# Ten of twelve heads' q, k, v by seven products of halves, turned back on TensorE

## The chip, the cores and the metric

One core of a Trainium2 chip runs one launch of the kernel. The metric is the device time of that launch in microseconds, the median of three runs. TensorE is called PE below, VectorE DVE, ScalarE ACT, GpSimd POOL and SyncE SP.

## What is computed

One decoder layer over 2048 tokens of width 1024, in fp32. The parts that the change touches, cut from the reference:

```python
h = (rms_norm(x, norm_w) * (1.0 + scale[:, None]) + shift[:, None]).astype(dt)
z = h @ w_in                      # 1024 x 10240
a, b, g_conv, q, k, v, g_attn, m_conv, m_attn = jnp.split(z, SPLIT_POINTS, axis=-1)
u = depthwise_causal_conv(a * jax.nn.sigmoid(b), conv_w, conv_b)      # 31 taps
...
q = rope(rms_norm(q, q_norm_w).astype(dt), positions)      # 12 heads of 128
k = rope(rms_norm(k, k_norm_w).astype(dt), positions)
for g, (window, dilation) in enumerate(((128, 1), (512, 4), (2048, 16))):
    sl = slice(g * HEADS_PER_GROUP, (g + 1) * HEADS_PER_GROUP)        # four heads
    o_g, l_g = dilated_window_attention(q[:, :, sl], k[:, :, sl], v[:, :, sl], window, dilation)
...                               # the groups merged by softmax of l_g, then gates and projections
```

## The kernel before

**The input h.** The rows of x are normalised, transposed on PE and kept in SBUF as "quarters": 4 blocks of 128 channels by 512 tokens, each as a high part and a low part (`hT_hi`, `hT_lo`). A product of two fp32 matrices is three matmuls: high by high, high by low, low by high. h is also written to memory (`h_d`).

**Stage one: units.** A unit `u` is one head. `GROUPS = (1, 2, 0)`: units 0 to 3 have dilation 4, units 4 to 7 dilation 16, units 8 to 11 dilation 1. For each unit and each block `j` of 128 tokens, `project_step` issues 24 matmuls of 128 x 384 (eight channel blocks by three terms, line 371) into one PSUM bank `pz`, which holds q, k and v of the block with tokens on partitions. Then ACT squares q and k for the norm (L388), POOL takes the inverse root (L114, L115), DVE scales (L402) and turns by the angles (L409 to L412). Units 0 to 7 write the block to memory (`qkv_d`) and their attention reads it back with a stride (`lqk`, `lv`); units 8 to 11 use it from SBUF.

Two places as they stand, the terms of a block's 24 matmuls and the seven products of a quad:

```python
        terms = [(k, a, w[k]) for k in range(KC) for a, w in ((hi, wh), (hi, wl), (lo, wh))]
...
            nc.tensor.matmul(pz[:, :width], part(a, k, P * j, P), w[:, :width], start=(m == 0), stop=(m == 23))
...
    PRODUCTS = (("A11", "B11"), ("A12", "B21"), ("S2", "T2"), ("S1", "T1"), ("S3", "T3"), ("S4", "B22"), ("A22", "T4"))
...
            terms = [t for k in range(4) for t in ((wh[:, k], ah[:, k]), (wh[:, k], al[:, k]), (wl[:, k], ah[:, k]))]
```

**Attention.** A block of attention has four steps, five in group 0: transposing q and k (`ptq`, L436), scores (`ps`, L451) with the softmax on DVE and ACT (L461, L463), transposing the weights (`ptp`, L468), times v (`po`, L500), and, where u is 8 or more, the merging of the three groups (`weigh`, L476 to L484) and the turn of the result (`pta`, L491). One step per projection step, inserted between its matmuls, is what `Flow` deals out. The tags z, s, o and t of the PSUM pool have two banks each; all eight are used.

**Stage two: quads.** The rest of `w_in` is computed with channels on partitions, for pairs of 128-column blocks, in two halves of 1024 tokens. One pair and one half is a job, or quad: seven products of quarters instead of eight (`PRODUCTS`), 12 matmuls of 128 x 512 each (L897), with ACT copying partial results out of PSUM (L903) and DVE and POOL adding. One product of one job is called a slot. 22 jobs per half: 12 gates, 2 of the attention gate, 8 of the convolution's input (`ab`); 44 jobs, 308 slots. `column_steps` loads the four weight blocks, forms the differences and splits them into high and low (L860 on ACT, L861 on DVE or POOL), seven slots ahead. In the first half the differences are stored (`t_d`), in the second read again. The sums of quarters of h come from `s_d`; between the halves, two jobs at a time are run alternately while the quarters of the second half land and are split (L725, L726). The 31-tap convolution runs on DVE beside the quads: `run_conv` emits 2.9 of its 800 small steps per slot in the first half, 3.1 in the second.

**Stage three.** The output projections of attention (`ya`) and convolution (`yc`), and the last projection by seven products (`oa`, `ob`, `oc`).

PE's order is the program's own, written out by hand (`tc.manual_schedule`). On the other engines a planner orders instructions by its estimate of when they can run; each engine then works its list strictly in that order.

Of the kernel before, what the change touches and what calls it, by code (L numbers as in the profile page):

```python
# [54 lines left out]
def tile_hybrid_block(  # L55
# [19 lines left out]
    def bank(tag, name):  # L75
        return psum.tile([P, 512], F32, tag=tag, name=name)

    qkv_d = {u: dram.tile([S, 3, P], F32, name=f"qkv{u}_d") for u in range(2 * NH)}
# [10 lines left out]
    wo_d = dram.tile([7, 4, P, 512], F32, name="wo_d")  # L89
# [144 lines left out]
    def part(x, k, t0, w, nk=1):  # L234

        q = x[k // 4, t0 // 512]
        ks = k % 4 if nk == 1 else slice(k % 4, k % 4 + nk)
        return q[:, ks, t0 % 512 : t0 % 512 + w]
# [137 lines left out]
    def tokens_tiles(n):  # L376

        return wk.tile([P, 2, P], F32, tag="lqk", name=f"lqk{n}", bufs=3), wk.tile([P, P], F32, tag="lv", name=f"lv{n}", bufs=8)

    def project_step(u, j, cs, wts, hooks, hold=False):  # L380

        n = f"{u}_{j}"
        pz = bank("z", f"pz{n}")
        z_tokens(pz, 384, *wts, j, hooks, u == 0 and j == 0)
        sq = wk.tile([P, P], BF16, tag="sq", name=f"sq{n}", bufs=1)
        st = wk.tile([P, 8], F32, tag="sta", name=f"st{n}", bufs=4)
        for i in range(2):
            nc.scalar.activation(sq, pz[:, P * i : P * i + P], AF.Square, scale=1.0 / math.sqrt(P),  # L388
                                 accum_out=st[:, i : i + 1])
        if GROUPS[u // NH]:  # L390
            qkv = wk.tile([P, 3, P], F32, tag="qkv", name=f"qkv{n}")
            tq, tv = qkv[:, :2], qkv[:, 2]
        elif hold:
            held = wk.tile([P, 3, P], F32, tag="qkv", name=f"qkv{n}")
            tq, tv = qkv = held[:, :2], held[:, 2]
        else:
            tq, tv = qkv = tokens_tiles(n)
        nc.scalar.activation(tv, pz[:, 256:384], AF.Copy)
        rsqrt_cols(st[:, 2:4], st[:, 0:2], 2, st[:, 4:6])
        qk = wk.tile([P, 4, 64], F32, tag="qk", name=f"qk{n}", bufs=1)  # L400
        for i in range(2):
            nc.vector.scalar_tensor_tensor(qk[:, 2 * i : 2 * i + 2].rearrange("p a b -> p (a b)"),  # L402
                                           pz[:, P * i : P * i + P], st[:, 2 + i : 3 + i], wqk[:, i, :],
                                           op0=ALU.mult, op1=ALU.mult)
        t3 = wk.tile([P, 2, 2, 64], F32, tag="t3", name=f"t3{n}", bufs=1)
        t1 = tq.rearrange("p a (b c) -> p a b c", b=2)
        cosb = cs[:, j, 0, :][:, None, :].to_broadcast([P, 4, 64])
        sinb = cs[:, j, 1, :][:, None, :].to_broadcast([P, 4, 64])
        nc.vector.tensor_tensor(t3.rearrange("p a b c -> p (a b) c"), qk, sinb, op=ALU.mult)  # L409
        nc.vector.tensor_tensor(t1.rearrange("p a b c -> p (a b) c"), qk, cosb, op=ALU.mult)  # L410
        nc.vector.tensor_sub(t1[:, :, 0, :], t1[:, :, 0, :], t3[:, :, 1, :])
        nc.vector.tensor_add(t1[:, :, 1, :], t1[:, :, 1, :], t3[:, :, 0, :])  # L412
        return qkv

    def strided(u, j):

        src = qkv_d[u].rearrange("(n i r) a c -> r n i a c", n=4, r=4)[j // 4, j % 4] if GROUPS[u // NH] == 1 else \
            qkv_d[u].rearrange("(i r) a c -> r i a c", r=16)[j]
        qk, v = tokens_tiles(f"{u}_{j}")
# [4 lines left out]
    def attend_step(u, j, qkv, state, hold=False):  # L424
# [8 lines left out]
        def turn_qk():  # L433
            pt = bank("t", f"ptq{n}")
            for i in range(2):
                nc.tensor.transpose(pt[:, P * i : P * i + P], qk[:, i], ident)  # L436
            if g == 0 and not hold:
                fetch()
            if hold:
                qkT = wk.tile([P, 3, P], F32, tag="qkv", name=f"qkT{n}")[:, :2]  # L440
            else:
                qkT = wk.tile([P, 2, P], F32, tag="qkT", name=f"qkT{n}", bufs=3)
            nc.scalar.activation(qkT.rearrange("p a b -> p (a b)"), pt[:, :256], AF.Copy)  # L443
            box["kv"] = ([] if first or hold else [state["prev"]]) + [(qkT, v)]
# [3 lines left out]
        def scores():  # L448
            ps = bank("s", f"ps{n}")
            for i, (kt, _) in enumerate(box["kv"]):  # L450
                nc.tensor.matmul(ps[:, P * i : P * i + P], box["q"][:, 0, :], kt[:, 1, :], start=True, stop=True)  # L451
            o = box["o"] = wk.tile([P, ACC_W], F32, tag="osb", name=f"osb{n}", bufs=5)
            if g == 0:
                st = box["st"] = mp.tile([P, 5, NG], F32, tag="stm", name=f"stm{n}", bufs=4)
                if hold:
                    fetch()
# [3 lines left out]
            sm = box["sm"] = wk.tile([P, 256], F32, tag="sm", name=f"sm{n}")  # L460
# [4 lines left out]
        def turn_p():  # L465
            pt = bank("t", f"ptp{n}")
            for i in range(nk):
                nc.tensor.transpose(pt[:, P * i : P * i + P], box["sm"][:, P * i : P * i + P], ident)  # L468
            pT = box["pT"] = wk.tile([P, 256], F32, tag="pT", name=f"pT{n}")
# [16 lines left out]
        def turn_o():  # L486
            if j % 2 == 0:
                return
            pt = bank("t" if u == NG * NH - 1 and j in (13, 15, 1, 3) else "o", f"pta{n}")
            for b, o in enumerate((state["even"], box["o"])):  # L490
# [630 lines left out]
    for at in range(7):  # L1121
        prepare(at)
# [451 lines left out]
```

## Time and profile before

| | |
|---|---|
| median of three runs | 2398.8 us (2398.56 to 2399.97) |
| profiled execution | 2401.62 us, its span 2399.8 us |
| stage one, heads | about 46 to 1099 us |
| stage two, quads | 1099 to 1960 us |
| stage three | 1960 to 2400 us |
| mean granted PE clock | 0.993 |
| moved by DMA | 378.6 MB, 158 GB/s over the span |

PE's busy time is a sum of overlapping instructions, so the spacing between starts is what counts. The stage limits are read from the first and last instructions of the lines named above.

### The profile page before, as it was taken

The page shows a single profiled execution, that of the slowest core. Times are in us where ns is not written, and L with a number is a line of the kernel's source. Part 1 is how long each engine was busy: PE and PEld are TensorE (multiplying, and loading weights), DVE is VectorE, ACT ScalarE, POOL GpSimd, SP SyncE. Part 2 cuts the span into 40 slices and gives each one's busy share as a digit, 9 for nine tenths or more (in the row PEclk, how much of TensorE's full clock was granted, in tenths as well). Part 3 has the DMA queues.
Part 4 walks back from the last instruction along what each step waited for, and adds up shares of the span by engine and source line. Part 5 has one row for each costly group of instructions (what it writes and reads, how often), then busy time and mean ns, then how long its engine had stood idle before and what let it go on. Part 6 is the DMA issues. An engine that isn't in the chain of part 4 may idle for free.

```text
span 2399.8 us, 38725 instructions
## 1 busy us (share of the span) xinstructions
PE 2356.1 (98%) x12353; PEld 2089.2 (87%) x12353; DVE 1738.8 (72%) x4091; ACT 1022.4 (43%) x2850; POOL 842.7 (35%) x1003
## 2 busy tenths in 40 slices
PE   6999999999999999999999999999999999999999
PEld 2989999999999999998888888788888888878887
DVE  5865655655556777777699999979968778787544
ACT  4733433333444454456444444644444444332221
POOL 3421111111111111123667779656556730000221
PEclk8999999999999999999999999999999999999999
DMA  7633544555552222134545455745444579866552
GB/s 258 216 118 105 163 124 143 155 151 155 165 161 79 65 79 62 55 108 156 169 133 176 154 158 193 239 127 152 141 149 132 167 228 319 288 230 200 177 158 101
DMA packets 354105, 378.56 MB, mean 158 GB/s; under 512 B 29736, under 2 KB 251208, under 8 KB 353902
## 3 DMA queue, kind: packets, MB, share of 16 engines
q1 hardware_dynamic: 316414, 316.64, 42.4%
q10 hardware_dynamic: 37488, 59.46, 7.3%
q8 instruction: 98, 1.61, 0.3%
q14 instruction: 105, 0.86, 0.1%
HBM read 235.34 MB, written 140.64 MB: 157 GB/s over the span
## 4 chain that ended last, share of the span: by engine, by line
PE 87%; DVE 3%; DMA 2%; ACT 2%; issue 1%; POOL 1%; SPq 0%; ACTq 0%; DVEq 0%; POOLq 0%
PE pz L371 29%; PE paab L897 7%; PE yc L1203 6%; PE oa L1485 4%; PE ya L1203 4%; PE pcab L897 4%; PE pag_mc_d L897 4%; PE pag_g_d L897 3%; PE pag_ma_d L897 3%; PE po L500 3%; PE ps L451 3%; PE oc L1485 2%; PE pcg_g_d L897 2%; PE pcg_mc_d L897 2%; PE paag L897 2%; PE pbab L897 2%
## 5 line engine op out<-in xcount | busy, mean ns | idle before, releaser
L371 PE MATMUL pz<-wh_u,hT_lo 128*128 128x384 f32 x1536 | 536.8, 350 | 5.4 <-DVE hT_lo L290 3.6
L371 PE MATMUL pz<-wh_u,hT_hi 128*128 128x384 f32 x1536 | 518.7, 338 | 4.8 <-ACT wh_u L347 2.4
L371 PE MATMUL pz<-wl_u,hT_hi 128*128 128x384 f32 x1536 | 519.2, 338 | 0.4 <-DVE wl_u L350 0.4
L114 POOL TENSOR_SCALAR st<-st 128x2 f32<-128x2 f32 x192 | 48.6, 253 | 809.8 <-ACT sq L388 809.8
L402 DVE SCALAR_TENSOR_TENSOR qk<-pz,st,wqk 128x128 f32<-128x128 f32 x384 | 116.9, 346 | 270.7 <-POOL st L115 269.6
L371 PEld LDWEIGHTS pz<-wh_u,hT_hi 128*128 128x128 f32 x1536 | 291.0, 189 | 8.0 <-ACT wh_u L347 3.3
L371 PEld LDWEIGHTS pz<-wh_u,hT_lo 128*128 128x128 f32 x1536 | 290.0, 189 | 8.3 <-DVE hT_lo L290 4.6
L371 PEld LDWEIGHTS pz<-wl_u,hT_hi 128*128 128x128 f32 x1536 | 290.0, 189 | 1.6 <-DVE wl_u L350 1.1
L443 ACT ACTIVATE qkT<-ptq 128x256 f32<-128x256 f32 x192 | 73.5, 383 | 358.3 <-PE ptq L436 304.0
L975 DVE SCALAR_TENSOR_TENSOR ce<-us,pair_taps,ce 128x512 f32<-128x512 f32 x240 | 180.6, 753 | 6.5
L946 DVE SCALAR_TENSOR_TENSOR ce<-ut,chan,ce 128x512 f32<-128x512 f32 x240 | 178.7, 745 | 0.0
L861 POOL TENSOR_TENSOR slT<-wT,shT 128x512 fp32r<-128x512 f32 x107 | 143.7, 1344 | 81.0 <-ACT shT L860 81.0
L959 DVE SCALAR_TENSOR_TENSOR cq<-ut,chan,cq 128x512 f32<-128x512 f32 x208 | 155.2, 746 | 1.0
L860 ACT ACTIVATE shB<-wB 128x512 fp32r<-128x512 f32 x130 | 82.0, 631 | 162.7 <-PE paab L897 51.7
L115 POOL TENSOR_TENSOR st<-st,mhalf 128x2 f32<-128x2 f32 x192 | 137.3, 715 | 16.0
L388 ACT ACTIVATE sq<-pz 128x128 bf16<-128x128 f32 x384 | 105.6, 275 | 87.5 <-PE pz L371 78.5
L860 ACT ACTIVATE shT<-wT 128x512 fp32r<-128x512 f32 x110 | 69.4, 631 | 163.9 <-POOL wT L852 33.3
L861 POOL TENSOR_TENSOR slB<-wB,shB 128x512 fp32r<-128x512 f32 x85 | 111.0, 1306 | 77.9 <-ACT shB L860 77.4
L500 PE MATMUL po<-lv,pT 128*128 128x128 f32 x596 | 96.8, 274 | 0.0
L500 PEld LDWEIGHTS po<-lv,pT 128*128 128x128 f32 x596 | 90.9, 190 | 0.6 <-issue 0.5
L409 DVE TENSOR_TENSOR t<-qk,tab 128x256 f32<-128x256 f32 x192 | 82.4, 429 | 5.5
L861 POOL TENSOR_TENSOR slT<-wB,shT 128x512 fp32r<-128x512 f32 x57 | 75.1, 1322 | 27.5 <-ACT shT L860 27.4
(742 smaller groups left out, 6162.2 us busy)
## 6 DMA issues: line engine op xcount, KB each, us to landing
wB<-in_w_in_dram SPq DMA_DIRECT2D x154, 256.0 KB, 3.4
qkv_d<-qkv SPq DMA_DIRECT2D x128, 192.0 KB, 2.3
wT<-tT_d SPq DMA_DIRECT2D x88, 256.0 KB, 2.7
raw_u<-in_w_in_dram SPq DMA_DIRECT2D x93, 192.0 KB, 3.4
tT_d<-wB ACTq DMA_DIRECT2D x66, 256.0 KB, 2.3
lqk<-qkv_d SPq DMA_DIRECT2D x128, 128.0 KB, 2.2
acc_d<-osb SPq DMA_DIRECT2D x128, 65.0 KB, 2.0
part<-acc_d ACTq DMA_DIRECT2D x64, 130.0 KB, 2.2
```

Source lines behind the costliest of these rows:

```text
L115: nc.gpsimd.tensor_tensor(dst, scratch[:, :n], mhalf[:, :n], op=ALU.pow)
L371: nc.tensor.matmul(pz[:, :width], part(a, k, P * j, P), w[:, :width], start=(m == 0), stop=(m == 23))
L402: nc.vector.scalar_tensor_tensor(qk[:, 2 * i : 2 * i + 2].rearrange("p a b -> p (a b)"), pz[:, P * i : P * i + P], st[:, 2 + i : 3 + i], w ...
L500: nc.tensor.matmul(po[:, :P], box["pT"][:, P * i : P * i + P], vt, start=(i == 0), stop=(i == nk - 1))
L860: nc.scalar.activation(h, q[name], AF.Copy)
L861: eng.tensor_tensor(l, q[name], h.bitcast(F32), op=ALU.subtract)
L897: nc.tensor.matmul(ps, w, x, start=(m == 0 and ps.name not in first), stop=(m == 11 and not more), skip_group_check=True)
L946: stt(box["e"], e[:, 1 + j : 513 + j], chan[:, cb, 2 * j : 2 * j + 1], box["e"], op0=ALU.mult, op1=ALU.add)
L959: stt(box["o"], o[:, 2 + j : 514 + j], w, psum_o, op0=ALU.mult, op1=ALU.add)
L975: stt(dst, box["both"][:, 1 + j : 513 + j], pair_taps[:, cb, j : j + 1], box["e"], op0=ALU.mult, op1=ALU.subtract if j == 0 else ALU.add)
L1203: nc.tensor.matmul(pz, w, xx, start=(m == 0), stop=(m == len(terms) - 1))
L1485: nc.tensor.matmul(ps, y, w, start=(m == 0 and ps.name not in begun), stop=(m == 11 and not more), skip_group_check=True)
```

## The change

Only units 0 and 1 are still projected block by block (`DIRECT = 2`). For the other ten heads, 30 blocks of 128 columns become 15 pairs: for two heads, v with v, then q with k of each. They are run as quads, in two rounds: all 15 for tokens 1024 to 2047, then all 15 for tokens 0 to 1023. The gates and `ab` jobs follow for the first half and then the second, so there are 74 jobs and 518 slots.

- A head quad gives q, k, v with channels on partitions, so `turn_back` transposes them on PE in pairs of token blocks (four 128 x 128 transposes into one bank), and `finish_qk` does norm and angles for two blocks at once. Results of all heads go to memory, and all attention is read from memory.
- In the first round the split weights (high and low) are written to memory, 512 KB for each product; in the second round they are read back and not split again. That is 7 x 15 pieces.
- Attention steps and turns are dealt out by `hook`, called twice in each slot, ahead of the sixth and of the last of its 12 matmuls. A block's steps are two hooks apart (`GAP = 2`). Blocks start at 0.25 per hook in the first round, none from slot 91 to 118, then at most one per hook as the heads become ready. All of it must be done by slot 237 (`TAIL`), after which the convolution begins at 3.1 steps per slot, 3.3 in the second half.
- Landing of the other half's quarters now happens twice: at slot 91 and at slot 350. The first uses three landing buffers.
- Until `TAIL`, `pb` and `pc` of a quad share one PSUM bank of tag s, the turns have the other, and the banks of tags o and t serve all attention steps of one hook together.
- The gate row (`gate_*`) and the sums of quarters for the first half move into these slots; those for the second half (`early_sums`) are formed during unit 1. Look-ahead of the weights is six slots instead of seven.

```diff
-            for p in range(NB):
-                j = (p + 3) % NB if last_unit else p
+    DIRECT = 2
+    for u in range(DIRECT):
+        for p in range(NB):
+            j = (p + 12) % NB if u else p
...
+            project_step(u, j, cur, extra)
...
+    def turn_back(pair):
+
+        pz = bank("s", f"zt{pair[0][1]}{pair[0][2][0]}_{pair[0][3]}", 1) if lone() else bank("o", f"zt{pair[0][1]}{pair[0][2][0]}_{pair[0][3]}")
+        for a, e in enumerate(pair):
+            for i, z in enumerate(e[4:6]):
+                nc.tensor.transpose(pz[:, 256 * a + P * i : 256 * a + P * i + P], z, ident)
...
+    def finish_qk(n, j, nb, pz, to):
...
+        if nb == 2:
+            src = qk.rearrange("p a b -> p (a b)")
+            nc.scalar.activation(src, pz, AF.Copy)
+            pz = src
+        for i in range(nq):
+            nc.scalar.activation(sq, pz[:, P * i : P * i + P], AF.Square, scale=1.0 / math.sqrt(P),
+                                 accum_out=st[:, i : i + 1])
+        rsqrt_cols(st[:, 4 : 4 + nq], st[:, 0:nq], nq, st[:, 8:12])
+        for i in range(nq):
+            nc.vector.scalar_tensor_tensor(qk[:, 2 * i : 2 * i + 2].rearrange("p a b -> p (a b)"),
+                                           pz[:, P * i : P * i + P], st[:, 4 + i : 5 + i], wqk[:, i % 2, :],
+                                           op0=ALU.mult, op1=ALU.mult)
...
+        nc.vector.tensor_tensor(by_block(tq), by_block(t3), cosb, op=ALU.mult)
+        nc.vector.tensor_tensor(by_block(t3), by_block(t3), sinb, op=ALU.mult)
+        nc.vector.tensor_sub(tq[:, 0::2], tq[:, 0::2], t3[:, 1::2])
+        nc.vector.tensor_add(tq[:, 1::2], tq[:, 1::2], t3[:, 0::2])
...
-        def turn_qk():
-            pt = bank("t", f"ptq{n}")
+        def turn_qk(get):
+            pt = get("t")[:, 256:]
             for i in range(2):
                 nc.tensor.transpose(pt[:, P * i : P * i + P], qk[:, i], ident)
...
+        steps = []
+        for f in (turn_qk, scores, turn_p, values) + ((turn_o,) if g == 0 else ()):
+            steps += [f, *[lambda get: None] * (GAP - 1)]
...
             for m, (w, x) in enumerate(terms):
+                if m in ((3, 7, 11) if 201 <= slot[0] < 201 else (5, 11)):
+                    hook(m > 5)
                 nc.tensor.matmul(ps, w, x, start=(m == 0 and ps.name not in first), stop=(m == 11 and not more),
...
+    heads = []
+    for u in range(DIRECT, NG * NH, 2):
+        heads += [("v", (u, u + 1)), ("q", (u,)), ("q", (u + 1,))]
+    heads.insert(-3, heads.pop(-3))
...
+    def hook(late_half):
+        at = slot[0]
+        if at >= TAIL:
+            return
...
+        ready = sum(e[0] <= at for e in turned)
+        since[0] += 1
+        if ready > 1 and since[0] >= (3 if lone() else 2):
+            since[0] = 0
+            pair = [turned.pop(0) for _ in range(2)]
+            readers.append(turn_back(pair))
...
+        readers += [f(get) for f in main.turn()]
+        for f in readers:
+            if f:
+                f()
+        credit[0] = min(credit[0] + rate(at), 1.5)
+        if order and credit[0] >= 1 and len(waiting) < 3 and is_ready(*order[0], at):
+            credit[0] -= 1
+            u, j = order.pop(0)
+            waiting.append([2, u, j, strided(u, j)])
...
+    def lone():
+        return not any(a <= slot[0] < a + 28 for a in (begin[s1 - 2], begin[s3 - 2]))
+
+    def rate(at):
+        return 0.25 if at < begin[s1 - 2] else 0.0 if at < begin[s1] + 14 else 1.0
...
-        due += 2.9 if i < half_jobs - 2 else 1.5 if i < half_jobs + 2 else 3.1
-        count = int(due)
-        due -= count
-        run_conv(count)
+        if at > TAIL:
+            due += 3.1 if i < s3 - 2 else 1.5 if i < s3 + 2 else 3.3
+            count = int(due)
+            due -= count
+            run_conv(count)
```

In the added code `s1`, `s2` and `s3` are the numbers of the first job of the second head round, of the gates of the first half and of the second half (15, 30, 52), and `begin` gives the slot at which a job starts: `begin[s1 - 2]` is 91, `begin[s1]` 105, `begin[s3 - 2]` 350.

More of the change, by code (lines that the diff above doesn't have):

```diff
@@ L726, in quarter_split @@
         i2 = eng.tensor_tensor(l, raw, h.bitcast(F32), op=ALU.subtract)
-        if half == 0 and name == "S4":
+        if name == "S4" and eng is nc.vector and cols.stop - cols.start == 512 and s4_pinned[0]:
             tc.keep_in_program_order(i1)
@@ L915, in quad @@
         yield
+        pc = bank("s" if narrow else "o", f"pc{name}", 0 if alone else None)
         product(3, pc, True)
```

525 lines of the change are left out of this document (287 added, 238 removed).

## The prediction, on record before the changed kernel ran

> **What bounds the kernel now.** I read the page first, then the engines by stretches, then the chain of waits in order of time. The page:
>
> ```profile
> span 2399.8 us, 38725 instructions
> PE 2356.1 (98%) x12353; PEld 2089.2 (87%) x12353; DVE 1738.8 (72%) x4091; ACT 1022.4 (43%) x2850; POOL 842.7 (35%) x1003
> PE 87%; DVE 3%; DMA 2%; ACT 2%; issue 1%; POOL 1%; SPq 0%; ACTq 0%; DVEq 0%; POOLq 0%
> ```
>
> PE is busy 98% and carries 87% of the chain that ended last. Busy time overlaps between instructions, so prices must come from spacings. Four stretches (length, then busy time of PE, PEld, DVE, ACT, POOL with their instructions, then granted clock, DMA share, GB/s): the attention of group 0, the convolution beside the first half of the quads, the change of halves, the start of the last stage.
>
> ```profile
> 742.00:1096.00 354.00, 352.86 (x2340) 350.33 (x2341) 264.30 (x1080) 182.15 (x735) 66.05 (x180) 1.00 0.27 76
> 1200.00:1500.00 300.00, 299.43 (x1321) 247.69 (x1320) 281.43 (x408) 126.79 (x224) 230.21 (x188) 1.00 0.50 163
> 1500.00:1545.00 45.00, 40.55 (x167) 33.01 (x166) 43.50 (x57) 29.99 (x58) 31.17 (x22) 0.92 0.83 261
> 1960.00:2050.00 90.00, 90.00 (x402) 72.94 (x401) 66.17 (x107) 34.92 (x57) 2.90 (x4) 1.00 0.97 324
> ```
>
> PE has no gap worth the name except at the change of halves. DVE is second: 75% in group 0's attention, 94% under the convolution. The chain of waits gives lengths of unbroken matmul runs (start, length):
>
> ```profile
> 572.97 4.19 PE pz L371 x24
> 1261.53 5.44 PE pag_mc_d L897 x24
> 1536.12 5.49 PE paab L897 x12
> ```
>
> The first is one block of one unit, 24 matmuls of 384 columns, 0.174 us each. The second is two slots of a quad: 12 matmuls of 512 columns take 2.72 us, 0.227 each. The third is a slot that took double; I come back to it. PE's timeline in an attention step (start, length of the merged row):
>
> ```profile
> 800.81 0.34 PE L371 MATMUL pz<-wl_u,hT_hi 128*128 128x384 f32 x1
> 800.99 0.61 PE L500 MATMUL po<-lv,pT 128*128 128x128 f32 x4
> 801.43 0.38 PE L468 MATMUL ptp<-ident,sm 128*128 128x128 f32 x2
> 801.65 0.39 PE L451 MATMUL ps<-qkT,qkT 128*128 128x128 f32 x2
> 801.87 0.39 PE L451 MATMUL ps<-qkT 128*128 128x128 f32 x2
> 802.09 0.38 PE L436 MATMUL ptq<-ident,lqk 128*128 128x128 f32 x2
> 802.23 0.42 PE L371 MATMUL pz<-wh_u,hT_lo 128*128 128x384 f32 x1
> 802.49 0.34 PE L371 MATMUL pz<-wh_u,hT_hi 128*128 128x384 f32 x1
> ```
>
> From 800.81 to 802.49 are 1.68 us: two matmuls of 0.174 and twelve small fp32 ones, 0.111 us each, transposes and products alike, with no extra price for the break.
>
> **PE's own sum.** Removed: 10 heads x 16 blocks = 160 runs of about 4.18 us, 668.8 us. Added: 15 pairs x 2 rounds x 7 products = 210 slots of 2.72 us, 571.2 us. Added: for each pair and round 8 token blocks of 2 heads' columns, 16 transposes, 480 in all, x 0.111 = 53.3 us. The attention's own PE instructions stay the same. Sum: 571.2 + 53.3 - 668.8 = **-44.3 us**. That is the ceiling of the gain, since seven eighths of the columns are left but each must be turned. Everything else is a question of what stays hidden.
>
> **Where cover gets thin.** Group prices (busy sum, mean ns; then idle before, and what ended it), DVE and then ACT, one DMA issue on ACT and POOL's split:
>
> ```profile
> L975 DVE SCALAR_TENSOR_TENSOR ce<-us,pair_taps,ce 128x512 f32<-128x512 f32 x240 | 180.6, 753 | 6.5
> L402 DVE SCALAR_TENSOR_TENSOR qk<-pz,st,wqk 128x128 f32<-128x128 f32 x384 | 116.9, 346 | 270.7 <-POOL st L115 269.6
> L409 DVE TENSOR_TENSOR t<-qk,tab 128x256 f32<-128x256 f32 x192 | 82.4, 429 | 5.5
> L461 DVE CUSTOM_DVE_ANT_0 sm<-ps,mask 128x256 f32<-128x256 f32 x108 | 44.6, 414 | 0.0
> L470 DVE COPY pT<-ptp 128x256 f32<-128x256 f32 x108 | 44.5, 413 | 0.0
> L861 DVE TENSOR_TENSOR slB<-wB,shB 128x512 fp32r<-128x512 f32 x45 | 37.3, 828 | 21.1 <-ACT shB L860 20.9
> L484 DVE SCALAR_TENSOR_TENSOR part<-part,stm 128x128 f32<-128x128 f32 x64 | 22.8, 357 | 9.5 <-ACT part L483 9.0
> L502 DVE SCALAR_TENSOR_TENSOR osb<-po,stm,part 128x128 f32<-128x128 f32 x64 | 21.9, 344 | 0.4 <-PE po L500 0.4
> L683 DVE TENSOR_TENSOR sx<-sx,sx 128x512 f32<-128x512 f32 x32 | 21.8, 683 | 0.0
> L479 DVE TENSOR_TENSOR stm<-stm 128x3 f32<-128x3 f32 x64 | 10.4, 162 | 26.6 <-ACT stm L478 23.9
> ...
> L388 ACT ACTIVATE sq<-pz 128x128 bf16<-128x128 f32 x384 | 105.6, 275 | 87.5 <-PE pz L371 78.5 <-DVE wT L852 2.1
> L860 ACT ACTIVATE shB<-wB 128x512 fp32r<-128x512 f32 x130 | 82.0, 631 | 162.7 <-PE paab L897 51.7 <-PE pag_mc_d L897 31.0 <-PE pag_g_d L897 22.6
> L443 ACT ACTIVATE qkT<-ptq 128x256 f32<-128x256 f32 x192 | 73.5, 383 | 358.3 <-PE ptq L436 304.0 <-DVE pT L470 39.8 <-DVE lqk L412 6.8
> L463 ACT ACTIVATE sm<-sm,stm 128x256 f32<-128x256 f32 x60 | 30.4, 506 | 11.5 <-DVE stm L461 11.5
> L483 ACT ACTIVATE part<-part,stm 128x128 f32<-128x128 f32 x64 | 25.5, 400 | 5.9 <-DVE stm L482 5.5 <-ACT spare_hi L1023 0.4
> ...
> 802.08 0.33 ACTq L516 DMA_DIRECT2D part<-acc_d  x1
> ...
> L861 POOL TENSOR_TENSOR slT<-wT,shT 128x512 fp32r<-128x512 f32 x107 | 143.7, 1344 | 81.0 <-ACT shT L860 81.0
> ```
>
> *The attention's tail.* Following `hook` and `is_ready` by hand through the slots: 32 blocks start before slot 70, none until 129, the other 160 in slots 129 to 231, because a head of the second round is complete only some eight slots after its quad. 53 of group 0's 64 blocks fall into the 35 slots 196 to 230, with 12 pairs of q and k to finish, two head quads and three gate quads. There:
> PE: 35 x 2.72 + 53 x 13 x 0.111 + 48 x 0.111 = 95 + 76 + 5 = 177 us.
> DVE: a block costs 0.414 (scores) + 0.413 (copy) + 5 x 0.162 (small ones) + 0.357 + 0.344 = 2.34; a pair 4 x 0.346 + 2 x 0.683 + 2 x 0.429 = 3.61 (its 512-wide multiplications priced at L683). 53 x 2.34 + 12 x 3.61 + 10 sums x 0.683 + 6 splits x 0.828 = 179 us. Between the small ones it waits for ACT's exponential, 26.6/64 = 0.42 a block, 22 us if nothing fills it.
> ACT: a block 0.383 + 0.506 + 0.400 + 2 x 0.275 + 0.33 for the issue = 2.17; a pair 0.631 + 4 x 0.275 = 1.73; 53 x 2.17 + 12 x 1.73 + 55 copies of 512 x 0.631 + 24 issues x 0.33 = 178 us.
> All three are full, where before this attention ran at 75% DVE. 94% is the highest DVE share at which the trace shows PE unhurt, and 179/0.94 = 190: **+14 us**. Ends: +2 (DVE perfectly packed, 179), +37 (waits unfilled as well, 201/0.94 = 214). I take 14 since the planner did fill 94% under the convolution.
>
> *The second landing.* At the change of halves PE waits once and then runs a slot at half speed (who waited for whom: total, times, longest):
>
> ```profile
> PE paab L897 <- ACT spare_hi L1023: 4.4, 1, 4.4
> ```
>
> 4.4, and 5.49 - 2.72 = 2.8 in the slot that took double: 7.2 us. The change has this event twice, the new one with three landing buffers. **+7 us**; 0 if the planner hides it, 20 if ACT stands behind several late landings.
>
> *The old passage from units to quads* disappears. There PE stood 2.0 us for a bank and resumed at 0.42 instead of 0.227 a matmul:
>
> ```profile
> 1104.75 0.44 PE L436 MATMUL ptq<-ident,lqk 128*128 128x128 f32 x2 [2.00 <-DVE pT L470]
> 1104.95 0.62 PE L897 MATMUL pbg_g_d<-hT_hi,first_w 128*128 128x512 f32 x1
> 1105.37 0.63 PE L897 MATMUL pbg_g_d<-hT_lo,first_w 128*128 128x512 f32 x1
> ```
>
> The attention that held the bank is gone, but first weights must still arrive at slot 0. **-3 us** (-5 to 0).
>
> *Convolution.* The same 800 steps get 280 slots instead of 295; 0.2 more per slot x 0.753 = 0.15 us on 281.43/300 x 2.72 = 2.55: 2.70 of 2.72. **+3 us** (0 to 8).
>
> *First round.* In each stretch of seven slots in which q and k are finished, DVE has 4 x 3.61 + 3 x 0.828 + 2 x 0.683 + 3.5 blocks x 1.17 (0.414, 0.413, 0.344) = 22.4 us; PE 19 + 16 x 0.111 + 3.5 x 11 x 0.111 = 25. Covered. But a 512-wide subtraction that costs 0.683 beside the units (L683; POOL at 66.05/354 in the stretch shown) costs 0.828 at L861, where POOL is at 230/300; here POOL has nine pieces of about 1.34 a job, half its time. **+2 us** (0 to 10). [...]
>
> *Step distance.* A step came once per block, over 5 us apart; now two hooks, about 3.4 us in the first round and 5.5 in the tail, with DVE bursts of 3.6 us ahead of it. `pb` must be read within one slot since `pc` takes its bank. What hides it is the planner's order. **+3 us** (0 to 15).
>
> Gate row, sums of quarters and the doubled weight traffic I cost at nothing. The first are 32 DVE operations in slots with spare DVE. In the first round a slot of about 3.6 us moves 512 KB of split weights, about 146 KB of raw ones, 150 KB of q, k, v and 130 KB for attention, some 270 GB/s; at 324 GB/s PE was busy 90.00 of 90. On SP's queue the weights are issued six slots ahead, so a store that waits for DVE delays them within that lead; without it each slot would see a landing.
>
> Sum: -44.3 + 14 + 7 - 3 + 3 + 2 + 3 = **-18.3 us**. Against the profiled execution's span of 2399.8 us (1.8 us around it, and 2.8 above the median of the runs) this is 2381.5; applied to the median 2398.8 it gives **2381 us**.
>
> **The rivals.** *Tail bound by DVE, slower:* in slots 196 to 230 its waits stay unfilled and the two banks of tags o and t make PE stand for each hook: 214 instead of 177, +37. Pauses then reach 2 us, and the rows at 1104.75 show that such a one is followed by half speed; six of them at 2 us more are +12. With the other terms (+12) the total is -44.3 + 37 + 12 + 12 = +17, 2416 us. It decides once the tail's loss exceeds 32 us. For it: three full engines; against it: 94% was carried without loss. Chance 0.24. A landing at its upper end together with the step distance gives the same sign, 2405; chance 0.06.
> *Full cover:* DVE packs the tail, the landing hides: 2354 us. Chance 0.09.
> *Clock:* group 0's hooks put 14 small fp32 instructions after six large ones, over half of PE's time. The trace granted 1.00 from 742 to 1096 with such bursts a quarter of the time. If the share counted, half speed over the tail would add 177 us at most, about 2560; chance 0.04. [...]
> *Nothing gained:* losses of 40 to 49 leave no measurable change, within 0.2% (about 4.8 us, what a measurement of this kernel can tell from none): 0.09.
>
> **How the numbers follow.** Forecast, 5 to 35 us faster: 0.48. Faster 0.48 + 0.09 = 0.57, same 0.09, slower 0.34. The range goes from full cover, 2354, into the slower cases to 2422, which leaves out the clock and the worst landings.
>
> **What would show it.** Right: 210 new slots of 2.72 us, 480 transposes at 0.111, PE gaps only at slots 91 to 112 and 196 to 231, DVE above 90% there. Wrong: a granted clock below 0.97, PE waiting for DVE in the first round, runs of 12 matmuls longer than 2.72 outside those places, or PE standing at turns for their bank.

## The result and the profile after

The changed kernel takes 2468.6 us, median of four runs (2464.97 to 2472.47), beside 2398.7 for the kernel before on the same chip (2396.47 to 2399.97). The ratio is 1.0293, 95% interval 1.0274 to 1.0311: slower by 70 us where the prediction said faster by 18, and beyond the upper end of its range, 2422.

The page of the kernel after, its span and the busy times:

```profile
span 2465.4 us, 37563 instructions
PE 2353.1 (95%) x11513; PEld 1948.4 (79%) x11513; DVE 1836.6 (74%) x3822; ACT 1167.1 (47%) x3041; POOL 1041.9 (42%) x1011
PE 65%; DVE 14%; DMA 10%; ACT 5%; issue 4%; POOL 3%; SPq 1%; POOLq 0%; DVEq 0%; ACTq 0%
```

In the chain that ended last PE fell from 87% to 65%; DVE rose from 3% to 14% and DMA from 2% to 10%: PE now stands for other engines and for transfers. The number of PE's instructions moved as the prediction had it: 12353 - 160 x 24 + 210 x 12 + 480 = 11513.

To see where PE stands we summed, stretch by stretch, the time from each of its instructions' start to the next one's, less the spacing that each has in an unbroken run (0.227, 0.174 or 0.111 us by width). We call the sum **PE's loss**; it holds standing still and half-speed matmuls (0.43 us apart after the wait at 497.11, below) alike. What is left is PE's own time: 2304.6 us before, 2261.9 after, so PE's work fell by **42.7 us**. This figure is made of instruction counts times these spacings. The loss rose from 91.8 to about 199.5 us. Together the two changes make up, to within a microsecond, the 65.6 us by which the spans of the two traces differ (2465.4 and 2399.8). By stretch:

| stretch of the kernel after | us | loss | the same places before |
|---|---|---|---|
| first two heads as units | 150 to 222 | 10.3 | 150 to 1140: 14.4 in all |
| first round, slots 0 to 90 | 222 to 586 | **55.8** | |
| landing, 91 to 117 | 586 to 684 | 18.7 | |
| second round, 118 to 195 | 684 to 1024 | 9.4 | |
| attention's tail, 196 to 230 | 1024 to 1235 | **31.8** | |
| quads beside the convolution | 1235 to 1561 | 1.4 | 0.9 |
| second landing | 1561 to 1604 | 5.4 | 7.5 |
| all the rest | | 67 | 69 |

The engines in these stretches, from the first round on (length, then busy times as in the prediction, granted clock, DMA share, GB/s):

```profile
222.00:586.00 364.00, 329.72 (x1633) 268.62 (x1634) 257.14 (x474) 186.24 (x534) 203.38 (x176) 0.96 0.82 275
586.00:684.00 98.00, 85.34 (x378) 69.40 (x377) 72.11 (x128) 54.77 (x165) 47.49 (x43) 0.92 0.77 264
684.00:1024.00 340.00, 336.72 (x2009) 292.07 (x2008) 189.57 (x689) 181.98 (x653) 51.86 (x74) 1.00 0.81 244
1024.00:1235.00 211.00, 191.12 (x1184) 162.19 (x1183) 173.85 (x682) 142.56 (x507) 81.41 (x122) 0.98 0.63 191
1235.00:1561.00 326.00, 325.25 (x1437) 268.56 (x1436) 280.99 (x429) 142.21 (x248) 244.15 (x201) 1.00 0.50 164
1561.00:1604.00 43.00, 38.10 (x169) 31.22 (x167) 42.23 (x59) 27.84 (x52) 35.35 (x25) 1.00 0.72 230
```

The first and third rows are the same sort of work, quads with q, k, v to finish. PE is busy in 329.72 of 364 us of the one and in 336.72 of 340 of the other. DVE is no fuller than 71% in either; what differs most is POOL: 203 us busy in the first, 52 in the third, where the stored weights are read again.

Groups of DVE's instructions between 225 and 580 us, after, and then the matching scaling of the kernel before in the same window:

```profile
L394 DVE SCALAR_TENSOR_TENSOR qkq<-qkq,stq,wqk 128x128 f32<-128x128 f32 x112 | 71.0, 692 | 9.0 <-POOL stq L118 8.9
L403 DVE TENSOR_TENSOR qkq<-qkq,tab 128x512 f32<-128x512 f32 x28 | 26.2, 935 | 0.6
```

```profile
L402 DVE SCALAR_TENSOR_TENSOR qk<-pz,st,wqk 128x128 f32<-128x128 f32 x134 | 40.8, 346 | 142.7 <-POOL st L115 142.7
```

The same 128x128 scaling takes 692 ns instead of 346 by the mean. The median is still 347: in slots 0 to 90, 38 of the 112 scalings take over 600 ns, up to 1452, and none of them lies between 400 and 600. So most are unhurt and a third are far longer. The scaling used to read PSUM (`pz`); now it reads ACT's copy in SBUF (`qkq`) beside `wqk` in SBUF. The timeline of the kernel after shows one pair of heads (start, length of the merged row):

```profile
490.17 1.68 POOL L832 TENSOR_TENSOR wB_make<-wB_make,wB_make 128x512 f32<-128x512 f32 x1 [0.38 <-DVE sB_make L846]
490.61 5.27 DVE L394 SCALAR_TENSOR_TENSOR qkq<-qkq,stq,wqk 128x128 f32<-128x128 f32 x4
...
491.93 1.26 POOL L832 TENSOR_TENSOR wT<-wB_make,wB_make 128x512 f32<-128x512 f32 x1
...
493.15 1.31 POOL L832 TENSOR_TENSOR wB_make<-wB_make,wB_make 128x512 f32<-128x512 f32 x1
494.43 1.30 POOL L846 TENSOR_TENSOR sB_make<-wB_make,sB_make 128x512 fp32r<-128x512 f32 x1
...
496.00 0.41 DVE L490 CUSTOM_DVE_ANT_0 sm<-turn_o_False,mask 128x256 f32<-128x256 f32 x1
...
496.45 0.51 ACT L492 ACTIVATE sm<-sm,osb 128x256 f32<-128x256 f32 x1 [4.32 <-DVE osb L490]
...
497.11 0.69 PE L497 MATMUL turn_t_False<-ident,sm 128*128 128x128 f32 x2 [5.02 <-ACT sm L492]
...
497.88 1.20 PE L891 MATMUL pav<-S_hi,sT_make 128*128 128x512 f32 x2
```

Four scalings take 5.27 us, about as long as the four POOL subtractions beside them, 5.55. The softmax's first step stands behind them in DVE's list (the last of its scores' matmuls takes 0.39 us from 488.48, the step starts at 496.00), ACT's exponential waits for it, and PE waits 5.02 us at its turn. Its next large matmuls start 0.43 us apart instead of 0.227. Where POOL pauses, the four take 1.13 us:

```profile
636.02 1.13 DVE L394 SCALAR_TENSOR_TENSOR qkq<-qkq,stq,wqk 128x128 f32<-128x128 f32 x4
```

PE's waits between 225 and 690 us carry it on (total, times, longest):

```profile
PE turn_t_False L497 <- ACT sm L492: 17.4, 10, 5.0
PE turn_o_False L531 <- DVE pT L502: 7.4, 6, 2.7
PE ztq L422 <- ACT qkq L387: 7.0, 2, 6.7
PE pcv L891 <- DVE spare_lo L904: 5.8, 2, 3.2
```

### The profile page after: what moved, and what is told of

It reads as the page before. It is cut to its first block, busy times and chain, and to the rows that moved or that the text cites. A ratio compares the mean times of both kernels' runs of the same rounds, so it can differ in the third digit from the quotient of the medians.

```text
span 2465.4 us, 37563 instructions
## 1 busy us (share of the span) xinstructions
PE 2353.1 (95%) x11513; PEld 1948.4 (79%) x11513; DVE 1836.6 (74%) x3822; ACT 1167.1 (47%) x3041; POOL 1041.9 (42%) x1011
## 3 DMA queue, kind: packets, MB, share of 16 engines
q8 instruction: 91, 1.49, 0.2%
## 4 chain that ended last, share of the span: by engine, by line
PE 65%; DVE 14%; DMA 10%; ACT 5%; issue 4%; POOL 3%; SPq 1%; POOLq 0%; DVEq 0%; ACTq 0%
PE yc L1337 7%; PE paab L891 7%; PE paq L891 4%; PE oa L1619 4%; PE pcab L891 4%; PE pag_g_d L891 4%; PE ya L1337 3%; DVE qkq L394 3%; PE pag_ma_d L891 3%; PE pcq L891 2%; PE pag_mc_d L891 2%; PE pav L891 2%; DMA part<-acc_d 2%; PE oc L1619 2%; PE pbab L891 2%
## 5 line engine op out<-in xcount | busy, mean ns | idle before, releaser
L846 POOL TENSOR_TENSOR sT_make<-wB_make,sT_make 128x512 fp32r<-128x512 f32 x108 | 148.1, 1372 | 108.3 <-ACT sT_make L845 99.6
L394 DVE SCALAR_TENSOR_TENSOR qkq<-qkq,stq,wqk 128x128 f32<-128x128 f32 x320 | 143.8, 510 | 52.4 <-POOL stq L118 51.9
L846 POOL TENSOR_TENSOR sT_again<-wT_again,sT_again 128x512 fp32r<-128x512 f32 x88 | 116.4, 1323 | 91.5 <-ACT sT_again L845 77.8
L832 POOL TENSOR_TENSOR wB_make<-wB_make,wB_make 128x512 f32<-128x512 f32 x72 | 96.5, 1341 | 58.2 <-DVE sB_make L846 53.6
L846 POOL TENSOR_TENSOR sB_again<-wB_again,sB_again 128x512 fp32r<-128x512 f32 x66 | 89.7, 1359 | 43.6 <-ACT sB_again L845 24.5
L390 ACT ACTIVATE sqq<-qkq 128x128 bf16<-128x128 f32 x320 | 98.1, 306 | 10.7 <-DVE stm L513 3.0
L374 PE MATMUL pz<-wh_u,hT_hi 128*128 128x384 f32 x256 | 90.3, 353 | 8.9 <-DVE qk L394 3.1
L374 PE MATMUL pz<-wh_u,hT_lo 128*128 128x384 f32 x256 | 89.2, 350 | 4.7 <-DVE hT_lo L293 4.6
L118 POOL TENSOR_TENSOR stq<-stq,mhalf 128x4 f32<-128x4 f32 x80 | 90.8, 1135 | 6.0
L374 PE MATMUL pz<-wl_u,hT_hi 128*128 128x384 f32 x256 | 89.5, 350 | 0.9 <-DVE wl_u L353 0.8
```

What stands on the lines that cost most here:

```text
L832: (nc.vector if first else nc.gpsimd).tensor_tensor(dst, x0, x1, op=ALU.subtract)
L846: eng.tensor_tensor(hl[:, 1], q[name], hl[:, 0].bitcast(F32), op=ALU.subtract)
```

## The experiments

**Theory A:** DVE instructions with two SBUF inputs and POOL's instructions exclude each other, whole instruction by whole instruction, and the changed scaling is newly exposed to this. **Rival B:** two hooks between the steps of attention are too few, whatever the scaling costs. The tail and the landing were tried beside them. Each ratio below is to the kernel before on the same chip in the same session.

**1. The scaling reads PSUM again (e1_psum).**

```diff
-        if nb == 2:
-            src = qk.rearrange("p a b -> p (a b)")
-            nc.scalar.activation(src, pz, AF.Copy)
-            pz = src
```

> The norm's squares and scaling of a pair read the turned q and k in PSUM, without the copy to SBUF. Theory A (exclusion: a DVE instruction with two SBUF inputs and a POOL instruction do not run side by side, so each scaling waits for a whole POOL instruction): the scaling's mean falls from 510 ns over the kernel (about 680 in the first head round) to about 350, the stretch from slot 0 to slot 91 falls from 361 us by 20 to 30, the whole kernel from 2468 to about 2435. Rival B (step distance: two hooks are too short for any burst of DVE work before them): the scaling may get shorter, but PE still stands for the softmax, slot 0 to 91 stays above 350 and the total above 2455; holding the bank longer may even add waits for the turns.

Measured: 2483.0 us (2478.0 to 2488.2), 1.0336 [1.0319, 1.0353]. DVE's group and PE's largest wait, 225 to 580 and 225 to 690 us:

```profile
L390 DVE SCALAR_TENSOR_TENSOR qkq<-ztq,stq,wqk 128x128 f32<-128x128 f32 x108 | 30.4, 344 | 28.0 <-POOL stq L118 27.8
```

```profile
PE ztq L418 <- DVE qkq L390: 43.3, 12, 6.5
```

The duration is back at 344 ns, as theory A says. But the kernel is slower, not faster: the bank with the turned q and k is now held until POOL's inverse root and DVE's scaling are done, and PE stands for it. The first round's loss is 68.2 us. ACT's copy, which exposes the scaling, is also what frees the bank; half of theory A's expectation failed. PE's waits for the exponential did fall, from 17.4 to 2.7 us, but the total is where rival B had put it, above 2455, so this run alone doesn't decide between the two.

**2. Four hooks between the first round's steps (e2_gap4).**

```diff
+        gap = 4 if slot[0] < begin[s1 - 2] else GAP
...
-            steps += [f, *[lambda get: None] * (GAP - 1)]
-        return steps[: len(steps) - GAP + 1]
+            steps += [f, *[lambda get: None] * (gap - 1)]
+        return steps[: len(steps) - gap + 1]
```

> Attention blocks that start in the first head round have their steps four hooks apart instead of two; nothing else changes. Rival B (step distance): PE's waits for the softmax (about 17 us) and for the copied weights (7) in slots 0 to 91 vanish, the stretch falls from 361 us to 330 or less, the total to about 2435. Theory A (exclusion with POOL): DVE's scaling stays at about 680 ns there, a part of the waits goes because there is time to bear them, but those for the one PSUM bank of the sums remain; the stretch falls by 10 to 20, the total to about 2450. Both expect the tail (slots 196 to 231) unchanged.

Measured: 2467.9 us, 1.0278 [1.0262, 1.0293]. PE's waits between 225 and 690 us: those for the exponential are gone, and others stand in their place:

```profile
PE pcq L892 <- DVE spare_hi L905: 9.4, 3, 5.2
PE ztq L422 <- ACT qkq L387: 8.0, 2, 7.2
PE pav L892 <- ACT spare_lo L898: 7.0, 4, 2.7
PE pcv L892 <- DVE spare_hi L905: 5.3, 1, 5.3
```

The first round still loses 52.6 us, so rival B, which had put the total at 2435, falls: a late DVE delays whatever PE needs next. Theory A's own figure for this run, 2450, was missed too.

**3. A part of POOL's work out (e3_nopool), then all of its weight work of the first round (e5_quiet).** Both replace POOL's low parts by a copy on ACT; the second also leaves out the differences of weights. The outputs of both lack these terms. The edit shown is e5_quiet's, with `quiet` true for the first round's quads; e3_nopool has the second hunk alone, for the head quads.

```diff
         def combine(name, dst, x0, x1):
+            if quiet:
+                q[name] = x0
+                return
...
-                eng.tensor_tensor(hl[:, 1], q[name], hl[:, 0].bitcast(F32), op=ALU.subtract)
+                if quiet and eng is nc.gpsimd:
+                    nc.scalar.activation(hl[:, 1], q[name], AF.Copy)
+                else:
+                    eng.tensor_tensor(hl[:, 1], q[name], hl[:, 0].bitcast(F32), op=ALU.subtract)
```

> In the first head round the low parts of the weights that POOL would form are left out: ACT writes a second copy of the raw weights in their place, so POOL has only the differences (four a job) and the sums. Theory A: the scaling's mean in the first round falls from 680 ns towards 450, slot 0 to 91 falls from 361 us by 20 or more although ACT has four more copies a job; total about 2445. Rival B and a rival C (ACT or DMA set the waits there): the stretch stays within 5 us of 361 or grows with ACT's 30 us of added work.

> All of POOL's work on weights in the first head round is left out: the differences are not formed (raw blocks stand for them) and ACT copies the raw blocks where POOL would form low parts. POOL keeps the root and one sum a job. Theory A (exclusion): the scaling's mean in slots 0 to 91 falls from 690 ns to about 360, DVE's bursts to 3.6 us, and what PE loses there, 56 us above the spacing of its instructions, falls to 15 to 25; total about 2430. Rival D (DVE's order and the step distance, with bursts of any length): the scaling gets short, but the loss stays above 38; total above 2448.

Measured: e3_nopool 2457.0 us, 1.0237 [1.0222, 1.0252], scaling 605 ns, the first round some 12 us shorter where 20 or more were expected; e5_quiet 2430.1 us (2427.0 to 2432.2), 1.0131 [1.0113, 1.0149], as expected. e5_quiet in 225 to 580 us and, as a window, 222 to 547:

```profile
L394 DVE SCALAR_TENSOR_TENSOR qkq<-qkq,stq,wqk 128x128 f32<-128x128 f32 x128 | 37.6, 355 | 21.7 <-POOL stq L118 21.7
```

```profile
222.00:547.00 325.00, 315.84 (x1634) 260.69 (x1634) 195.47 (x473) 210.26 (x588) 60.56 (x72) 1.00 0.93 314
```

With POOL quiet the scaling from SBUF takes 355 ns (1 of the 112 in slots 0 to 90 is over 600), the granted clock is 1.00 and the first round's loss falls from 55.8 to 16.3 us. ACT is busier than before and the DMA share higher (0.93), so neither was the cause.

**4. The same with four hooks (e7_quiet_gap4).**

> As the kernel with POOL's weight work of the first round left out, with the first round's attention steps four hooks apart as well. Theory A: little is left to gain, within 5 us of that kernel. Rival D: with short bursts and twice the distance the loss of slots 0 to 91 goes below 10 us, 10 or more under that kernel.

Measured: 2424.5 us, 1.0107 [1.0091, 1.0122]; the first round's loss is 11.0. That lies between the two expectations. The step distance is worth some 5 us here, beside 3 us of loss and nothing in the total in e2_gap4; both are little more than what separates one build from the next (see 6).

**5. The merging weights left out (e4_noweigh).** Group 0's `weigh` isn't called, so its output isn't merged with the other groups by their weights.

```diff
-            if g == 0:
-                weigh()
...
-                ... box["st"][:, 3, 0:1], box["part"][:, 0, :P] ...
+                ... box["st"][:, 1, 0:1], box["part"][:, 0, :P] ...
```

> The merging weights of group 0 are left out (six small DVE instructions, one on 128 columns, two on ACT, one on POOL per block); a fixed column of the block's state stands for the weight, the rows to merge are still loaded. Rival S (the tail is bound by the sum of DVE and ACT work and by the chain of small instructions): DVE loses 53 x 1.6 = 85 us of work and waits in slots 196 to 231, and the 32 us that PE loses there shrink below 10; total about 2443. Rival T (the banks that all steps of a hook share set the tail): the loss stays above 20 us, total above 2457. Theory A with the tail's own POOL work: between the two, since the scaling there averages 475 ns.

Measured: 2451.1 us, 1.0209 [1.0194, 1.0225]; the tail's loss is 13.5 instead of 31.8, between what the two rivals expected. The window 1025 to 1225 of the kernel after, then of e4_noweigh:

```profile
1025.00:1225.00 200.00, 180.44 (x1122) 153.37 (x1121) 165.86 (x648) 135.41 (x485) 78.17 (x116) 0.98 0.65 196
```

```profile
1025.00:1225.00 200.00, 193.73 (x1225) 168.89 (x1224) 123.60 (x348) 121.22 (x403) 70.73 (x67) 0.98 0.71 209
```

The tail is a separate price, and the merging is 18 of its 32 us. It has idle DVE time (165.86 of 200 us busy) while PE loses, so it isn't DVE's throughput alone.

**6. Six landing buffers (e6_ld6), and POOL's work on the gate quads under the tail left out (e8_quiet_gates).** The first is the whole computation: every second block of the first round's landing takes buffers from the tags `sm` and `pT`. The second is e5_quiet's edit with the condition `s2 <= i < s2 + 4`.

```diff
+            if i < s2 and k % 2:
+                for tag, c in (("sm", 0), ("pT", 256)):
+                    raw = wa.tile([P, 256], F32, tag=tag, name=f"landing0{name}_{k}_{c}", bufs=3)
+                    args = 0, name, k, slice(c, c + 256), raw
+                    quarter_load(*args)
+                    held.append((at + 2, lambda args=args, k=k: quarter_split(*args, nc.gpsimd if k == 3 else nc.vector)))
+                continue
```

> At the first landing every second piece goes to six idle half-size buffers of the attention's pool, so there are as many as six landing buffers instead of three; the computation is whole. Theory L (with three buffers SP stands behind the release of a buffer and ACT behind late landings): the loss in slots 91 to 118 falls from 19 us to 7 to 10, as at the old change of halves; total about 2457. Rival: DMA is full there (share about 0.8), landings are as late with more buffers, the loss stays above 15.

> For the four gate jobs ahead of slot 238 POOL's differences and low parts are left out as in the first round of the other kernel (ACT copies instead). Theory A for the tail: the scaling there falls from 475 ns to 360 and the loss of slots 196 to 231 from 32 us by 6 to 12, total about 2459. Rival S (the tail is the sum of DVE and ACT work with its chain): the loss stays within 4 us of 32 or grows, since ACT gets 16 more copies.

Measured: e6_ld6 2469.6 us (2466.5 to 2478.1), 1.0303 [1.0279, 1.0326], the landing's loss 11.2 instead of 18.7, but no lower total, where 2457 was expected. e8_quiet_gates 2471.8 us (2468.0 to 2479.1), 1.0310 [1.0288, 1.0332], the tail's loss 26.9 instead of 31.8, the scaling there 347 ns instead of 475, and no lower total either, where 2459 was expected. Losses of a stretch vary by a few microseconds from one build to the next (the first round gave 57.9 and 59.0 here, the landing 22.1 in e8_quiet_gates), which is as much as these two edits save. Alone they show nothing in the total.

**7. All of it together (e9_all).** e5_quiet's and e8_quiet_gates' conditions, e6_ld6 and e4_noweigh in one kernel.

> Left out: GpSimd's weight differences and low parts in the first round (as in e5_quiet) and in the four gate quads under the tail (as in e8_quiet_gates), and the merging weights of group 0 (as in e4_noweigh); a first-round landing has six buffers. Theory A with the tail as a second, separate loss: the prices add. From the changed kernel's 2468.6 we take 38 (first round), 18 (merging weights) and 0 to 10 (gates and landing): 2402 to 2413 us, within 15 us of the kernel before, with the first round's loss near 16 us, the tail's below 15 us. Rival (one delay that only moves: what is saved in one stretch is lost in the next): the total stays above 2420 us.

Measured: 2409.4 us (2402.6 to 2413.7, eight runs), 1.0035 [1.0022, 1.0047]. The prices add, as expected: first round 17.7, landing 17.1, tail 5.0. The landing kept its loss, so its expected gain isn't in the sum. Even without that work the kernel only comes near the one before. Its loss from 150 us to the tail's end is 57.5, beside 14.4 in the corresponding part before, and that takes back PE's 42.7.

**8. The whole computation, with POOL's share of the head weights on DVE (e10_dve), and that with four hooks and six buffers (e11_dve_gap4_ld6).** `vec` is true for the first round's quads.

```diff
-            (nc.vector if first else nc.gpsimd).tensor_tensor(dst, x0, x1, op=ALU.subtract)
+            (nc.vector if first or vec else nc.gpsimd).tensor_tensor(dst, x0, x1, op=ALU.subtract)
...
-            split(n, nc.vector if n in lo_engines else nc.gpsimd)
+            split(n, nc.vector if vec or n in lo_engines else nc.gpsimd)
```

> The whole computation. All differences and low parts of the head weights in the first round, which GpSimd computed, go to VectorE: some 8 operations a quad of about 0.69 us, 5.5 us more work for an engine that showed 191 us busy in 265, and 10.7 us less for GpSimd. [...] Rival C (VectorE is simply too full in the first round): the loss grows, the total is 2470 us or more.

> The whole computation. e10_dve with the first round's attention steps four hooks apart and six buffers for the first-round landing. Theory A: with the exclusion gone the two give what they gave before, some 5 us and 0 to 7 us: 2422 to 2440 us. Rival C: not below 2465 us. Neither theory expects it under the kernel before, since the tail's loss of about 32 us stays.

Measured: e10_dve 2438.6 us (2430.4 to 2442.0), 1.0164 [1.0147, 1.0181]; e11_dve_gap4_ld6 2434.8 us (2433.9 to 2436.0), 1.0143 [1.0128, 1.0158]. The window 222 to 555 us of e10_dve and its scaling:

```profile
222.00:555.00 333.00, 319.55 (x1633) 262.03 (x1632) 258.91 (x578) 187.14 (x535) 67.08 (x71) 0.99 0.90 302
```

```profile
L394 DVE SCALAR_TENSOR_TENSOR qkq<-qkq,stq,wqk 128x128 f32<-128x128 f32 x124 | 37.3, 362 | 7.2 <-POOL stq L118 7.1
```

DVE took over POOL's weight work, 104 more instructions than the kernel after has in its first round, and its busy time hardly rose: 258.91 us instead of 257.14. What it got in work it had been spending on waiting for POOL. The stretch is 31 us shorter and its loss 25.5 instead of 55.8. Rival C, which had put the total at 2470 or more, falls. (The trace is of e10_dve's fastest execution, 2430.4 us.) This is the clearest of the tests, since nothing is left out: 30 us come back only by taking work from the less busy engine and giving it to the busier one. These are the fastest whole versions of the change found, and both are still slower than the kernel before.

**9. The disputed cost by itself (e12_alone).** DVE and POOL on fixed tiles: for each of five kinds of DVE operation 48 in all (24 for the scaling from PSUM), and 74 POOL subtractions of 128x512, in one run.

> Not the block at all, only VectorE and GpSimd on fixed tiles, 24 VectorE operations a stage, alone or beside twelve GpSimd subtractions of 128x512 fp32. Theory A (whole instructions exclude each other): the scaling of 128x128 with two SBUF inputs takes about 0.28 to 0.35 us alone and over 0.9 us for each that meets a subtraction, since it waits out one; with its first input in PSUM it keeps its time, if one SBUF input is allowed beside GpSimd; the 512-wide multiplication goes from about 0.69 to over 1.3 us; a copy from PSUM keeps its time; GpSimd's subtraction goes from about 1.26 us alone to longer where it meets two-input operations. [...]

The planner mixed the stages, so tile names don't tell which ran beside what; the times do. From 18 to 88 us POOL works without a break; from 90 to 125 DVE works alone. One rotation beside POOL and one alone:

```profile
18.21 1.37 POOL L108 TENSOR_TENSOR pscaleP_beside<-pa,pb 128x512 f32<-128x512 f32 x1
18.38 1.34 DVE L83 SCALAR_TENSOR_TENSOR dscaleS_beside<-a,one,b 128x128 f32<-128x128 f32 x1
19.54 1.31 POOL L108 TENSOR_TENSOR pwideS_beside<-pa,pb 128x512 f32<-128x512 f32 x1
19.65 0.34 DVE L83 SCALAR_TENSOR_TENSOR dscaleP_beside<-ps,one,b 128x128 f32<-128x128 f32 x1
19.91 1.49 DVE L86 TENSOR_TENSOR dwideS_alone<-a,b 128x512 f32<-128x512 f32 x1
20.82 1.70 POOL L108 TENSOR_TENSOR pcopyP_beside<-pa,pb 128x512 f32<-128x512 f32 x1
21.32 1.75 DVE L86 TENSOR_TENSOR dwideS_beside<-a,b 128x512 f32<-128x512 f32 x1
22.48 1.70 POOL L108 TENSOR_TENSOR pcopyS_beside<-pa,pb 128x512 f32<-128x512 f32 x1
22.99 1.48 DVE L89 COPY dcopyS_beside<-a 128x512 f32<-128x512 f32 x1
```

```profile
91.75 0.34 DVE L83 SCALAR_TENSOR_TENSOR dscaleS_beside<-a,one,b 128x128 f32<-128x128 f32 x1
92.01 0.34 DVE L83 SCALAR_TENSOR_TENSOR dscaleP_beside<-ps,one,b 128x128 f32<-128x128 f32 x1
92.27 0.68 DVE L86 TENSOR_TENSOR dwideS_alone<-a,b 128x512 f32<-128x512 f32 x1
...
93.47 0.41 DVE L89 COPY dcopyS_beside<-a 128x512 f32<-128x512 f32 x1
```

The scaling with both tensors in SBUF takes 0.34 us alone and 1.34 beside POOL; with one in PSUM it takes 0.34 either way. The wide multiplication goes from 0.68 to 1.49 or 1.75. That every operation slows by one factor is ruled out: the factor is 4 for the short instruction and 2.2 to 2.6 for the long one, while the addition is about the same, 0.8 to 1.1 us, and follows what the POOL instruction has still to run when the DVE instruction starts, by the rows above 1.20 us at 18.38 (addition 1.0), 0.94 at 19.91 (0.81) and 1.20 at 21.32 (1.07).

## Why the prediction was wrong, point by point

**PE's own sum held.** Predicted -44.3, and -42.7 from the counts and these spacings. Whether the spacings hold in the new mix is what the trace adds: the 512-wide matmuls of the whole kernel are spaced 0.227 us by the median, and slots run at nearly the expected length, 2.72 (in the second round, in the chain of waits):

```profile
700.46 2.76 PE paq L891 x12
```

The 480 transposes are spaced 0.109 us by the median, beside 0.111 predicted. The granted clock in the second round is 1.00 with them. The clock rival put half speed over the whole tail, +177 us; the clock there is 0.98 and the loss 31.8, so it had no part in it. The lower clocks, 0.96, 0.92 and 0.98, are in the three stretches where PE waits.

**First round: the step that failed.** The prediction put +2 us here (0 to 10), and it measured +56. Of the 84 us between the predicted -18.3 and the traced +65.6, this step holds 54, the tail 18 and the landing 12; the smaller terms cancel. It compared 22.4 us of DVE work with 25 of PE work in seven slots and called that covered. It did see that DVE's instructions take longer beside POOL, and took this from two rows that were averages, 0.683 and 0.828 us, a factor of 1.21. The +2 is the author's estimate, and no run shows it. What the runs show is a loss of 55.8 us and, in e12_alone, an addition per instruction, 0.8 to 1.1 us, about the rest of a POOL instruction. It falls hardest on short ones: the four scalings alone went from 4 x 0.346 = 1.38 to 5.27 us at 490.61. And the engine totals were no test of cover: DVE works its list in order, so one burst of 5 us delays the softmax behind it (to 496.00 at the place shown), though DVE is at 71% over the stretch. e5_quiet and e10_dve give back 38 and 30 us of the total.

The wait goes both ways. In e12_alone POOL's subtraction takes 1.31 us at 19.54, beside the scaling from PSUM, and 1.70 at 20.82, where it starts within a wide multiplication. The four scalings at 490.61 last about as long as the four POOL instructions beside them, 5.27 and 5.55 us; a factor of 1.21 would have made 1.67 of their 1.38.

**The tail.** +14 predicted, within 2 to 37; measured 31.8. The mechanism was right only in part. The prediction expected DVE above 90% there; it was 173.85 of 211 us, 82%. The loss comes with idle DVE. PE's waits there are short, the longest 3.1 us, and most are for small DVE steps (`stm`) or the exponential, which points to the chain of short steps between DVE, ACT and PE. That the merging is 18 of it was shown (e4_noweigh); how the rest divides between exclusion and the distance of steps was not, since e8_quiet_gates changed the stretch by less than builds differ.

**The landing.** +7 predicted (0 to 20); 18.7 measured at the new landing, near the upper end. The trace shows the way that the prediction gave for that end, ACT standing behind late landings. The listed waits of PE from 586 to 684 us, 12.6 us, are all at the turns, and the longest is for ACT's copy of the turned q and k, whose bank PE needs; ACT's splits ahead of the copy waited for DMA:

```profile
648.84 0.63 ACT L729 ACTIVATE S_hi<-landing0S 128x512 fp32r<-128x512 f32 x1 [1.81 <-DMA landing0S<-s_d]
...
651.09 0.63 ACT L729 ACTIVATE A_hi<-landing0A 128x512 fp32r<-128x512 f32 x1 [1.62 <-DMA landing0A<-h_d]
...
651.62 0.58 ACT L387 ACTIVATE qkq<-ztq 128x512 f32<-128x512 f32 x1
...
652.26 1.11 PE L422 MATMUL ztq<-ident,spare_hi 128*128 128x128 f32 x4 [6.68 <-ACT qkq L387]
```

Six buffers took the loss to 11.2 in one trace, and left 17.1 in e9_all, where they are used too; with three it was about 13 in e5_quiet and 10 in e10_dve. What makes the pieces late stays open. The old landing cost 5.4 instead of 7.5.

**The smaller terms.** The convolution's +3 was nothing (1.4 beside 0.9). The old passage from units to quads is gone, as was said (its 6.7 us, where 3 was counted). The step distance, +3, cannot be told from the exclusion in the kernel as it is. The second round's 9.4 us and the units' 10.3 had no term.

**The rivals.** The slower one, a tail bound by DVE, gave 2416 by adding 49 us in the tail. The tail did lose 32, at that rival's point of decision; with the other terms as predicted this would have left no measurable change. The first round decided. None of the three slower rivals had the first round in it. The list of signs did name this one, "PE waiting for DVE in the first round", but as what would make the forecast wrong, without a price or a chance.

## What to carry to other kernels

Before a DVE operand is moved from PSUM to SBUF, ask what POOL does at that time: each DVE instruction with two SBUF inputs can then wait for most of a POOL instruction (0.8 to 1.1 us in e12_alone), and short ones multiply their time (0.34 us became 1.34). A group whose mean lies far above its median, 692 beside 347 ns here, can be a sign of it. Price contention per instruction and not by the ratio of two averages, and test cover by the longest burst ahead of the step that PE waits for, not by an engine's total. Where a stretch is lost to it, giving POOL's share to the busier DVE can be faster than sharing the work (30 us here).

## What was not expected of the hardware

A plain copy on DVE from SBUF to SBUF, with a single input, is excluded as well, which theory A as worded doesn't say: 128x512 fp32 took 0.41 us alone and 1.48 beside POOL in e12_alone. A 128x256 copy from PSUM isn't: its median is 0.42 us beside POOL (from 125.4 us on) and 0.42 alone (POOL idle, from 145.9 us on). Two groups between 90 and 140 us, where POOL works again from 125.4 on (shortest, median and longest in ns, first and last start):

```profile
L89 DVE COPY dcopyP_alone<-ps x14: 404/424/425, 125.4 to 131.3; 128x256 f32<-128x256 f32 x14
L89 DVE COPY dcopyS_beside<-a x13: 409/411/413, 90.8 to 122.7; 128x512 f32<-128x512 f32 x13
```
